# At the end of a sandwich layer: sums of squares by TensorE, products with high parts first, low parts after a half's updates

## The chip, the core and the metric

The kernel runs on one core of a Trainium2 chip. The metric is the device time of one execution in microseconds (us). An execution has one instruction queue for each engine: TensorE (PE) multiplies, VectorE (DVE) and ScalarE (ACT) work element by element, GpSimd (POOL) does a few additions and small powers, and SyncE (SP) issues most of the transfers. The engines wait for each other through semaphores. An engine takes its queue in order, so an instruction that waits holds up all those behind it.

## The reference, cut to what matters

The program is a chain of eight layers on x, 512 tokens of 1024 features in float32. The last four layers are "sandwiches", and the change is in how they end:

```python
def rmsnorm(x, g):
    y = x32 * lax.rsqrt(jnp.mean(x32 * x32, axis=-1, keepdims=True) + RMS_EPS)
    return (y * g.astype(jnp.float32)).astype(x.dtype)

def sandwich(x, g_pre, g_post, fn):
    return x + rmsnorm(fn(rmsnorm(x, g_pre)), g_post)
```

They are m0 (attention and convolution), f0 (feed-forward), m1 (attention and state space) and f1 (feed-forward). So the end of a layer needs a sum of squares of its own output over all 1024 features, then the update of x, and then, for the next layer, a sum of squares of the new x.

## The kernel before, in words

All of x lies in SBUF as eight tiles of 128 features by 512 tokens (`xs[0]` to `xs[7]`). A float32 product is made of three faster ones: a weight panel W is held as a high part `wh` and a low part `wl`, an activation as `xh` and `xl` (or `yh` and `yl`), and `mm3` adds wh·xh, wh·xl and wl·xh into the same PSUM tile (in the trace these are the products named g<-xh,wh, g<-xl,wh and g<-xh,wl). `panel` does that for the eight feature tiles k: 24 products for one weight panel of 128 output features.

Weight panels lie in the pool `pw`: three buffers each for `wh` and `wl`. `wchunk` takes a buffer and loads a panel; a panel that was split in an earlier layer comes by two transfers of SP, `wh<-preh` and `wl<-prel`. A transfer starts when the last reader of the old panel in its buffer is done.

`sandwich_end` (line 965) is the end of a layer. Its last three output panels are made in two halves of 256 tokens (`one`, `two`), so that the norm of half one can be worked out while half two is multiplied. In the order of the code, which PE and DVE keep here (`pinned[0] = (PE, V)`):

- `SumSq` collects the squares: ACT squares a tile (line 466), POOL adds it to `acc` (line 470), the last tile stays apart, and `sums` lets PE add over the 128 features with products of one column, a<-ones,acc and a<-ones,t.
- `factor` makes 1/sqrt from it, `diagonal` and `spread` bring it onto all partitions by two products a<-t,ones.
- `update(m, t, b)` scales the output tile, adds it to x on DVE, has ACT make `xh` (line 549), notes the square for later, and has DVE make the `xl` of the update before (`low`).
- The first three panels of the next layer, W0, W1 and W2, are multiplied with X in halves: W0 and W1 in turn for each k (`two_panels`), then W2. W0 to W2 are fetched as the buffers of this layer's last three panels come free.
- `panel_and_scales` (line 383) fetches W3 with the next free buffer, multiplies it for all 512 tokens, and makes the scale of the next norm after its first four k.

The last sandwich, f1, has no next layer (`srcs is None`): its updates go straight to the output.

Of the kernel before, what the change touches and what calls it, by code (L numbers as in the profile page):

```python
# [4 lines left out]
P = 128  # L5
NT = 512
D = 1024
KD = D // P
# [171 lines left out]
def build(nc, tc, A, out, stages=("a0", "b", "c", "a1", "m0", "f0", "m1", "f1")):  # L180
# [6 lines left out]
    AF = mybir.ActivationFunctionType  # L187
# [3 lines left out]
    V, S, G, PE = nc.vector, nc.scalar, nc.gpsimd, nc.tensor  # L191
# [3 lines left out]
    class Ordered:  # L195


        def __init__(self, eng):
            self.eng = eng
# [8 lines left out]
    PE, V = Ordered(PE), Ordered(V)  # L208
# [8 lines left out]
    def tl(pool, shape, tag, dt=F32, **kw):  # L217
        uid[0] += 1
        return pool.tile(list(shape), dt, tag=tag, name=f"{tag}_{uid[0]}", **kw)

    with ctx:
        pc = newpool(ctx, "pc")
# [22 lines left out]
        def psum_a():  # L245
            return tl(psa, (P, NT), "a")
# [206 lines left out]
        class SumSq:  # L453


            def __init__(self, n, apart=True):
                self.n, self.acc, self.rest, self.apart = n, None, {}, apart and n > 1

            def add(self, src, i, t=ALL, cls=False):
                if i == 0 and self.acc is None:  # L460
                    self.acc = tl(psm, (P, NT), "acc", bufs=1)
                sq = tmp() if i else self.acc
                if cls:
                    S.activation(classes(sq), tokens(src), AF.Square)
                else:
                    S.activation(sq[:, t], src, AF.Square)  # L466
                if i == self.n - 1 and self.apart:
                    self.rest[t.start] = sq
                elif i:
                    G.tensor_tensor(self.acc[:, t], self.acc[:, t], sq[:, t], op=ADD)  # L470

            def sums(self, t=ALL):

                ps = psum_a()
                n = (t.stop - t.start) // P
                for c in range(n):
                    o = t.start + c * P
                    both = [self.acc]
                    if self.apart:
                        both.append(self.rest[max(k for k in self.rest if k <= o)])  # L480
                    for i, a in enumerate(both):
                        PE.matmul(ps[:, c:c + 1], lhsT=a[:, o:o + P], rhs=ones[:, 0:1],
                                  start=i == 0, stop=i == len(both) - 1)
                return ps[:, 0:n]

        def small(n, tag):
            return tl(psm, (P, n), tag)

        neghalf = tl(pc, (P, 4), "neghalf")
        V.memset(neghalf, 0.5)  # L490
        S.activation(neghalf, neghalf, AF.Copy, scale=-1.0)
# [38 lines left out]
        state = {"first": None}  # L530

        def new_norm(row):
            state.update(row=row, X=[], ss=SumSq(KD, False))

        def finish_x(k, t=ALL, sq=True):

# [426 lines left out]


        def sandwich_end(W, Y, O, fresh, grow, srcs, pre=None, first=()):
            ss = SumSq(KD)
            kt = len(Y)
            nf = KD - 3

            def put(m, ps, t):  # L970
                if fresh:
                    ss.add(ps, m, t)
                    S.activation(O[m][:, t], ps, AF.Copy, scale=gcol(grow, m))
                else:
                    V.tensor_tensor(O[m][:, t], O[m][:, t], ps, op=ADD)
                    ss.add(O[m][:, t], m, t)
            first = list(first)
            for m in range(nf):
                put(m, first.pop(0) if first else gemm_T(W[m], Y), ALL)
            ch = [wchunk(W[m], kt * P) for m in range(nf, KD)]  # L980
            if pre is not None:
                s2 = small(4, "pc2")
                V.tensor_tensor(s2, pre, pre, op=MUL)

            def factor(t):
                c = small(2, "pc")
                if pre is None:
                    rstd(c, ss.sums(t), 1.0 / D, EPS)
                else:
                    a = slice(t.start // P, t.stop // P)  # L990
                    V.tensor_tensor(c, ss.sums(t), s2[:, a], op=MUL)
                    rstd(c, c, 1.0 / D, EPS)
                    V.tensor_tensor(c, c, pre[:, a], op=MUL)
                return c

            pss = {}

            def begin(m, t, k=None):
                pss[m] = psum_g()
                panel(pss[m], ch[m - nf], Y, t, range(kt if k is None else k))  # L1000

            def end(m, t, k):
                panel(pss[m], ch[m - nf], Y, t, range(k, kt))

            def done(m, t):
                put(m, pss[m][:, t], t)
            one, two = HALVES
            low, squares = [], []

            def add_squares():  # L1010
                while squares:
                    m, t = squares.pop(0)
                    state["ss"].add(xs[m][:, t], m, t)

            def update(m, t, b):
                o, x = O[m][:, t], xs[m][:, t]
                if fresh:
                    V.tensor_tensor(o, o, b, op=MUL)
                else:
                    V.scalar_tensor_tensor(o, o, gcol(grow, m), b, op0=MUL, op1=MUL)  # L1020
                (G if srcs is None and m % 3 == 2 else V).tensor_tensor(x, x, o, op=ADD)
                low.append(finish_x(m, t, False))
                if srcs:
                    squares.append((m, t))
                if len(low) > 1:
                    low.pop(0)()

            def last_low():
                low.pop(0)()
            a, b, c = range(nf, KD)  # L1030
            pinned[0] = (PE, V)
            for m in (a, b, c):
                begin(m, one)
                done(m, one)
            begin(a, two, kt - 4)
            f = factor(one)
            end(a, two, kt - 4)
            done(a, two)
            d1 = diagonal(f)
            if srcs:  # L1040
# [24 lines left out]
            ps = [psum_g() for _ in range(3)]  # L1065
            def two_panels(ks, t=one):
                for k in ks:
                    panel(ps[0], W0, X, t, [k])
                    panel(ps[1], W1, X, t, [k])
            two_panels(range(2))  # L1070
            update(4, one, b1)
            f = factor(two)
            update(5, one, b1)
            d2 = diagonal(f)
            add_squares()
            two_panels(range(2, 5))
            b2 = spread(d2)
            update(6, one, b1)
            update(7, one, b1)
            last_low()  # L1080
            add_squares()
            two_panels(range(5, KD))
            panel(ps[2], W2, X, one)
            for m in range(KD):
                update(m, two, b2)
                add_squares()
            last_low()
            two_panels(range(KD), two)
            panel(ps[2], W2, X, two)
            pinned[0] = (PE,)  # L1090
            p, sc, sb = panel_and_scales(srcs[3], X)
            state["first"] = ps + [p], sc, sb
            pinned[0] = ()
# [363 lines left out]
        def layer_m1(nxt):  # L1457
            with ExitStack() as c:
# [122 lines left out]
                V.tensor_tensor(t2[0:64], ps[64:128], t2[64:128], op=MUL)  # L1581
                V.tensor_tensor(kr[0:64], t1[0:64], t2[0:64], op=ADD)
                S.activation(kr[64:128], kr[0:64], AF.Copy)
                ss = SumSq(2)
                CQ = []
                for i in range(2):
                    ps = gemm_T(pre("m1_win", 4 + i), X)
# [165 lines left out]
```

## Time and profile before

| what | value |
|---|---|
| median of three runs | 2880.51 us (2877.24 to 2885.08) |
| the profiled execution | 2881.13 us, of which the span from the first to the last instruction is 2879.3 us |
| PE busy | 2812.2 us, 98% of the span |
| DVE, ACT, POOL busy | 1617.3, 1033.6, 215.4 us |
| mean granted TensorE clock | 0.991 |
| ends of m0, f0, m1, f1 in the trace | from about 1852, 2239, 2468 and 2848 us |

Starts are in us from the first instruction. A row of the timeline gives start, duration, engine, line, operation and tiles; in brackets stands how long the engine sat idle before it and what ended that. Durations of PE's rows overlap, since products are pipelined, so the distance between two starts tells what a product costs. A float32 product that isn't split stands as two rows (x2), and helpers record line 205 for most operations of PE and DVE, so the tile names tell which step it is. The granted clock is given as a share of full speed: TensorE has two levels, 1.2 and 2.4 GHz, and 0.51 to 0.57 in a short stretch means that the lower one held in nearly all of it.

### The profile page before, as it was taken

The page shows a single profiled execution, that of the slowest core. Times are in us where ns is not written, and L with a number is a line of the kernel's source. Part 1 is how long each engine was busy: PE and PEld are TensorE (multiplying, and loading weights), DVE is VectorE, ACT ScalarE, POOL GpSimd, SP SyncE. Part 2 cuts the span into 40 slices and gives each one's busy share as a digit, 9 for nine tenths or more (in the row PEclk, how much of TensorE's full clock was granted, in tenths as well). Part 3 has the DMA queues.
Part 4 walks back from the last instruction along what each step waited for, and adds up shares of the span by engine and source line. Part 5 has one row for each costly group of instructions (what it writes and reads, how often), then busy time and mean ns, then how long its engine had stood idle before and what let it go on. Part 6 is the DMA issues. An engine that isn't in the chain of part 4 may idle for free. (4 is left out here: it accounts for less than half of the span.)

```text
span 2879.3 us, 35015 instructions
## 1 busy us (share of the span) xinstructions
PE 2812.2 (98%) x13542; PEld 2320.6 (81%) x13542; DVE 1617.3 (56%) x3092; ACT 1033.6 (36%) x1661; POOL 215.4 (7%) x187
## 2 busy tenths in 40 slices
PE   8999999999999999999999998989999899999998
PEld 7888888888888888788888886778888756888886
DVE  4454654645455665654565488479754685343334
ACT  4322344444444432343323314443333325332222
POOL 2000010000000101220010100110000200200001
PEclk9999999999999999999999999999999999999999
DMA  4222332222222366555544352347773430423222
GB/s 157 95 88 95 121 109 96 81 88 95 74 96 89 128 205 207 183 191 161 160 163 161 123 193 94 114 171 257 278 254 106 170 137 19 143 92 101 97 94 68
DMA packets 127416, 385.48 MB, mean 134 GB/s; under 512 B 16144, under 2 KB 23057, under 8 KB 127249
## 3 DMA queue, kind: packets, MB, share of 16 engines
q1 hardware_dynamic: 107088, 325.57, 34.2%
q10 hardware_dynamic: 20160, 57.68, 5.4%
q8 instruction: 106, 1.74, 0.2%
q14 instruction: 62, 0.50, 0.1%
HBM read 312.94 MB, written 70.25 MB: 133 GB/s over the span
## 5 line engine op out<-in xcount | busy, mean ns | idle before, releaser
L320 ACT ACTIVATE wh<-wr 128x1024 fp32r<-128x1024 f32 (+2 forms) x408 | 421.6, 1034 | 1148.8 <-PE g L205 917.5
L205 DVE TENSOR_TENSOR wl<-wr,wh 128x1024 fp32r<-128x1024 f32 (+2 forms) x408 | 506.1, 1241 | 307.9 <-ACT wh L320 303.5
L205 PE MATMUL g<-xl,wh 128*128 128x512 f32 (+1 forms) x1720 | 659.1, 383 | 11.3 <-DVE xl L205 11.0
L205 PE MATMUL g<-xh,wh 128*128 128x512 f32 (+1 forms) x1720 | 662.9, 385 | 4.3 <-DMA wh<-preh 3.6
L205 PE MATMUL g<-xh,wl 128*128 128x512 f32 (+1 forms) x1720 | 657.4, 382 | 5.0 <-DMA wl<-prel 3.9
L205 PE MATMUL g<-yh,wh 128*128 128x512 f32 (+1 forms) x1046 | 393.4, 377 | 0.1
L205 PE MATMUL g<-wh,xh 128*128 128x512 f32 (+1 forms) x992 | 381.4, 385 | 9.8 <-ACT wh L320 9.8
L205 PE MATMUL g<-yl,wh 128*128 128x512 f32 (+1 forms) x1046 | 390.2, 373 | 0.0
L205 PE MATMUL g<-yh,wl 128*128 128x512 f32 (+1 forms) x1046 | 390.1, 373 | 0.0
L205 PEld LDWEIGHTS g<-xl,wh 128*128 128x128 f32 x1720 | 325.5, 189 | 75.5 <-DVE xl L205 15.3
L205 PEld LDWEIGHTS g<-xh,wl 128*128 128x128 f32 x1720 | 325.4, 189 | 69.6 <-DMA wl<-prel 4.9
L205 PEld LDWEIGHTS g<-xh,wh 128*128 128x128 f32 x1720 | 325.4, 189 | 65.8 <-DMA wh<-preh 4.6
L205 PE MATMUL g<-wl,xh 128*128 128x512 f32 (+1 forms) x992 | 376.7, 380 | 0.0
L205 PE MATMUL g<-wh,xl 128*128 128x512 f32 (+1 forms) x992 | 375.3, 378 | 0.0
L470 POOL TENSOR_TENSOR acc<-acc,t 128x256 f32<-128x256 f32 (+1 forms) x109 | 120.9, 1109 | 1721.4 <-issue 1406.9
L205 PEld LDWEIGHTS g<-yl,wh 128*128 128x128 f32 x1046 | 197.2, 189 | 36.1 <-issue 1.4
L205 PEld LDWEIGHTS g<-yh,wh 128*128 128x128 f32 x1046 | 197.0, 188 | 36.2 <-issue 1.4
L205 PEld LDWEIGHTS g<-yh,wl 128*128 128x128 f32 x1046 | 197.5, 189 | 34.3 <-DVE wl L205 0.4
L205 PEld LDWEIGHTS g<-wh,xh 128*128 128x128 f32 x992 | 187.7, 189 | 43.1 <-ACT wh L320 9.8
L205 PEld LDWEIGHTS g<-wh,xl 128*128 128x128 f32 x992 | 187.8, 189 | 34.3
L205 PEld LDWEIGHTS g<-wl,xh 128*128 128x128 f32 x992 | 187.9, 189 | 33.1 <-DVE wl L205 0.8
L205 DVE TENSOR_TENSOR t<-g,sb 128x512 f32<-128x512 f32 x112 | 77.1, 690 | 227.3 <-PE g L205 226.0
(309 smaller groups left out, 2679.1 us busy)
## 6 DMA issues: line engine op xcount, KB each, us to landing
wh<-preh SPq DMA_DIRECT2D x48, 512.0 KB, 3.8
wl<-prel SPq DMA_DIRECT2D x48, 512.0 KB, 4.3
wr<-in_f_wg_dram SPq DMA_DIRECT2D x40, 512.0 KB, 3.5
wr<-in_f_wu_dram SPq DMA_DIRECT2D x40, 512.0 KB, 3.5
preh<-ph ACTq DMA_DIRECT2D x39, 512.0 KB, 3.5
prel<-pl ACTq DMA_DIRECT2D x39, 512.0 KB, 6.5
wr<-in_a_wv_dram SPq DMA_DIRECT2D x32, 512.0 KB, 3.5
wr<-in_a_wu_dram SPq DMA_DIRECT2D x32, 512.0 KB, 3.7
```

The costliest lines, as they stand in the source:

```text
L205: r = f(*a, **k)
L320: S.activation(wh[:, :n], wr[:, :n], AF.Copy)
L470: G.tensor_tensor(self.acc[:, t], self.acc[:, t], sq[:, t], op=ADD)
```

## The change

Three things change at the sandwich ends.

- `SumSq(KD, 3)`: in the sum of squares of the layer's output, the last three tiles stay apart, not only the last one. PE's sum for 128 tokens then has four products of one column (acc and three tiles) where it had two.
- `PESums`: the squares of the new x are no longer added up by POOL. ACT squares each tile right after `xh`, and PE adds it at once: per tile and half two products of one column into one PSUM tile, which a product with `zeros` opens.
- `high` and `lows` take the place of `two_panels` and `panel`: for a half, all products with `xh` come first (for half one those of W0 and W1, then of W2; for half two all three panels in turn for each k), with the squares' products in between. `xl` is made only after all eight updates of the half, and all products with `xl` come last. All four remaining updates of half one stand ahead of the first product.

```diff
@@ class SumSq
-                if i == self.n - 1 and self.apart:
-                    self.rest[t.start] = sq
+                if i >= self.n - self.apart:
+                    self.rest.setdefault(t.start, []).append(sq)
@@
+        class PESums:
+            def __init__(self):
+                self.ps, self.n = psum_a(), 0
+                PE.matmul(self.ps[:, 0:4], lhsT=ones, rhs=zeros, start=True, stop=False)
+            def add(self, sq, t):
+                for o in range(t.start, t.stop, P):
+                    self.n += 1
+                    PE.matmul(self.ps[:, o // P:o // P + 1], lhsT=sq[:, o:o + P], rhs=ones[:, 0:1],
+                              start=False, stop=self.n == 4 * KD)
@@ def sandwich_end
-            ss = SumSq(KD)
+            ss = SumSq(KD, 3)
@@ def update
                 low.append(finish_x(m, t, False))
                 if srcs:
-                    squares.append((m, t))
-                if len(low) > 1:
-                    low.pop(0)()
+                    sq = tmp()
+                    S.activation(sq[:, t], x, AF.Square)
+                    squares.append((sq, t))
@@ the next layer's first panels
-            two_panels(range(2))
-            update(4, one, b1)
+            def high(t, ks, ns=range(3), sums=True):
+                for k in ks:
+                    for n in ns:
+                        for i in range(2):
+                            PE.matmul(ps[n][:, t], lhsT=W[n][i][:, k * P:(k + 1) * P], rhs=X[k][0][:, t],
+                                      start=k == 0 and i == 0, stop=False)
+                    if sums:
+                        state["ss"].add(*squares.pop(0))
+            def lows(t, ks):
+                for k in ks:
+                    for n in range(3):
+                        PE.matmul(ps[n][:, t], lhsT=W[n][0][:, k * P:(k + 1) * P], rhs=X[k][1][:, t],
+                                  start=False, stop=k == KD - 1)
+            state["ss"] = PESums()
+            for m in range(4, KD):
+                update(m, one, b1)
+            high(one, range(3), range(2))
             f = factor(two)
-            update(5, one, b1)
+            high(one, range(3, KD), range(2))
+            last_low(2)
             d2 = diagonal(f)
-            add_squares()
-            two_panels(range(2, 5))
+            high(one, range(2), [2], False)
             b2 = spread(d2)
-            update(6, one, b1)
-            update(7, one, b1)
-            last_low()
-            add_squares()
-            two_panels(range(5, KD))
-            panel(ps[2], W2, X, one)
+            high(one, range(2, KD), [2], False)
+            last_low(KD - 2)
+            lows(one, range(KD))
             for m in range(KD):
                 update(m, two, b2)
-                add_squares()
-            last_low()
-            two_panels(range(KD), two)
-            panel(ps[2], W2, X, two)
+            high(two, range(KD))
+            last_low(KD)
+            lows(two, range(KD))
```

PE's queue where the next layer's panels begin at the end of m0 (wh_14691 and wl_14692 are W0, wh_14738 is W1, xh_14725 and xl_14726 the first tile of the new x), before:

```order
L205 MATMUL g_14786<-xh_14725,wh_14691 128x256
L205 MATMUL g_14786<-xl_14726,wh_14691 128x256
L205 MATMUL g_14786<-xh_14725,wl_14692 128x256
L205 MATMUL g_14787<-xh_14725,wh_14738 128x256
L205 MATMUL g_14787<-xl_14726,wh_14738 128x256
L205 MATMUL g_14787<-xh_14725,wl_14739 128x256
```

and in the changed kernel (a_14796 is the PSUM tile of the sums, t_14731 the squares of the first tile, wh_14694 W0 and wh_14743 W1):

```order
L205 MATMUL a_14796<-zeros_112,ones_108 128x4
L205 MATMUL g_14793<-xh_14728,wh_14694 128x256
L205 MATMUL g_14793<-xh_14728,wl_14695 128x256
L205 MATMUL g_14794<-xh_14728,wh_14743 128x256
L205 MATMUL g_14794<-xh_14728,wl_14744 128x256
L205 MATMUL a_14796<-ones_108,t_14731 128x1 x2
```

The two products with xl have left this place, and two products of one column have come.

The last products of the stage and the first with W3 (wh_15049, 512 tokens), before. The row with wh_14691 or wl_14692 is the last use of W0's buffers, and W2 is wh_14782; between the dots stand 20 more products of W2:

```order
L205 MATMUL g_14786<-xl_14871,wh_14691 128x256
L205 MATMUL g_14786<-xh_14870,wl_14692 128x256
L205 MATMUL g_14787<-xh_14870,wh_14738 128x256
L205 MATMUL g_14787<-xl_14871,wh_14738 128x256
L205 MATMUL g_14787<-xh_14870,wl_14739 128x256
L205 MATMUL g_14788<-xh_14725,wh_14782 128x256
...
L205 MATMUL g_14788<-xh_14870,wh_14782 128x256
L205 MATMUL g_14788<-xl_14871,wh_14782 128x256
L205 MATMUL g_14788<-xh_14870,wl_14783 128x256
L205 MATMUL g_15053<-xh_14725,wh_15049 128x512
```

and in the changed kernel (W0, W1 and W2 are wh_14694, wh_14743 and wh_14789, W3 is wh_15076):

```order
L205 MATMUL g_14795<-xl_14815,wh_14789 128x256
L205 MATMUL g_14793<-xl_14822,wh_14694 128x256
L205 MATMUL g_14794<-xl_14822,wh_14743 128x256
L205 MATMUL g_14795<-xl_14822,wh_14789 128x256
L205 MATMUL g_15080<-xh_14728,wh_15076 128x512
```

Before, 28 products stand between the last read of W0's `wh` and the first one with W3; now there are two.

SP's queue at the same place, before (wh_15049 and wl_15050 are W3):

```order
L300 DMA pr_15212<-in_m_win_dram 128x1024
L316 DMA wh_15049<-preh_1533_7938 128x1024
L317 DMA wl_15050<-prel_1534_7939 128x1024
L254 DMA wr_15480<-in_f_wu_dram 128x1024
L254 DMA wr_15536<-in_f_wg_dram 128x1024
```

and in the changed kernel (wh_15076 and wl_15077):

```order
L300 DMA pr_15234<-in_m_win_dram 128x1024
L317 DMA wl_15077<-prel_1535_7941 128x1024
L316 DMA wh_15076<-preh_1534_7940 128x1024
L254 DMA wr_15502<-in_f_wu_dram 128x1024
L254 DMA wr_15558<-in_f_wg_dram 128x1024
```

The two transfers of W3 have changed places: the low part of W0 is now free first.

## Rows read from the trace of the kernel before

**Rows 1.** The page, part 1: busy time, share of the span, instructions.

```profile
PE 2812.2 (98%) x13542; PEld 2320.6 (81%) x13542; DVE 1617.3 (56%) x3092; ACT 1033.6 (36%) x1661; POOL 215.4 (7%) x187
```

**Rows 2.** PE's stage table, m0 then f0, m1: stretch, length, busy, clock.

```profile
1870.50:1897.10 26.60, 21.06 (x158) 1.00 0.27 95
1899.00:1903.00 4.00, 4.00 (x11) 0.57 0.95 297
2257.80:2261.20 3.40, 3.40 (x17) 0.51 0.16 64
2490.00:2497.00 7.00, 7.00 (x35) 0.52 0.17 65
2515.20:2519.00 3.80, 3.76 (x16) 1.00 0.68 245
```

**Rows 3.** Waits of PE in that stage: in total, times, longest.

```profile
PE g L205 <- DVE xl L205: 4.3, 6, 1.0
...
PE g L205 <- DVE xl L205: 4.1, 6, 0.8
...
PE g L205 <- DVE xl L205: 2.5, 4, 0.7
```

**Rows 4.** Timeline of PE: fetched panels, and the stage's borders.

```profile
1870.50 0.28 PE L205 MATMUL g<-xh,wh 128*128 128x256 f32 x1
1872.55 0.39 PE L205 MATMUL g<-xh,wl 128*128 128x256 f32 x1 [1.16 <-DMA wl<-prel]
1893.53 0.28 PE L205 MATMUL g<-xl,wh 128*128 128x256 f32 x1
1896.89 0.28 PE L205 MATMUL g<-xh,wl 128*128 128x256 f32 x1
1898.92 0.50 PE L205 MATMUL g<-xh,wh 128*128 128x512 f32 x1 [1.75 <-DMA wh<-preh]
2282.28 0.50 PE L205 MATMUL g<-xh,wh 128*128 128x512 f32 x1 [0.22 <-DMA wh<-preh]
2283.96 0.50 PE L205 MATMUL g<-xh,wl 128*128 128x512 f32 x1 [0.94 <-DMA wl<-prel]
2515.24 0.50 PE L205 MATMUL g<-xh,wh 128*128 128x512 f32 x1 [0.22 <-DMA wh<-preh]
```

**Rows 5.** Timeline of PE: one-column products at full and low clock; a spread.

```profile
1861.97 0.28 PE L205 MATMUL a<-ones,acc 128*128 128x1 f32 x2
1862.99 0.28 PE L205 MATMUL g<-yl,wh 128*128 128x256 f32 x1
1865.74 0.60 PE L205 MATMUL a<-t,ones 128*128 128x128 f32 x4
1866.10 0.36 PE L205 MATMUL g<-yh,wh 128*128 128x256 f32 x1
2490.58 0.42 PE L205 MATMUL a<-ones,acc 128*128 128x1 f32 x2
2492.14 0.56 PE L205 MATMUL g<-xh,wh 128*128 128x256 f32 x1
```

**Rows 6.** Timeline of SP: the transfer of W3's high part, in m0.

```profile
1893.85 0.32 SPq L316 DMA_DIRECT2D wh<-preh  x1
```

**Rows 7.** Timeline of DVE: an update; xl without and with POOL adding.

```profile
1866.38 0.42 DVE L205 TENSOR_TENSOR qkT<-qkT,a 128x256 f32<-128x256 f32 x1 [1.96 <-PE a L205]
1867.18 0.41 DVE L205 TENSOR_TENSOR qkT<-qkT,a 128x256 f32<-128x256 f32 x1
1875.35 0.48 DVE L205 SCALAR_TENSOR_TENSOR xl<-x,gains,xh 128x256 fp32r<-128x256 f32 x1
1877.35 0.94 DVE L205 SCALAR_TENSOR_TENSOR xl<-x,gains,xh 128x256 fp32r<-128x256 f32 x1
```

**Rows 8.** Timeline of POOL: additions into acc; of PE: f1's second sum.

```profile
1876.41 5.97 POOL L470 TENSOR_TENSOR acc<-acc,t 128x256 f32<-128x256 f32 x7 [0.98 <-POOL pc L498]
2863.95 0.38 PE L205 MATMUL a<-ones,t 128*128 128x1 f32 x2 [0.74 <-ACT t L466]
```

More of the change, by code (lines that the diff above doesn't have):

```diff
@@ L453, in build, with __init__ @@
         class SumSq:
-            def __init__(self, n, apart=True):
-                self.n, self.acc, self.rest, self.apart = n, None, {}, apart and n > 1
+            def __init__(self, n, apart=0):
+                self.n, self.acc, self.rest, self.apart = n, None, {}, apart
             def add(self, src, i, t=ALL, cls=False):
@@ L478, in sums @@
                     both = [self.acc]
-                    if self.apart:
-                        both.append(self.rest[max(k for k in self.rest if k <= o)])
+                    if self.rest:
+                        both += self.rest[max(k for k in self.rest if k <= o)]
                     for i, a in enumerate(both):
@@ L484, in sums @@
                 return ps[:, 0:n]
+        class PESums:
[7 more added lines that the diff above has]
+                              start=False, stop=self.n == 4 * KD)
+            def sums(self, t=ALL):
+                return self.ps[:, t.start // P:t.stop // P]
         def small(n, tag):
             return tl(psm, (P, n), tag)
+        zeros = tl(pc, (P, 4), "zeros")
+        V.memset(zeros, 0.0)
         neghalf = tl(pc, (P, 4), "neghalf")
@@ L532, in new_norm @@
         def new_norm(row):
-            state.update(row=row, X=[], ss=SumSq(KD, False))
+            state.update(row=row, X=[], ss=SumSq(KD))
         def finish_x(k, t=ALL, sq=True):
@@ L1007, in sandwich_end @@
             one, two = HALVES
[L1008 to L1013, printed above, removed]
+            low = []
             def update(m, t, b):
@@ L1023, in update, with last_low @@
                 if srcs:
-                    squares.append((m, t))
-                if len(low) > 1:
+                    sq = tmp()
+                    S.activation(sq[:, t], x, AF.Square)
+                    squares.append((sq, t))
+            squares = []
+            def last_low(n):
+                for _ in range(n):
                     low.pop(0)()
-            def last_low():
-                low.pop(0)()
             a, b, c = range(nf, KD)
@@ L1065, in sandwich_end @@
             ps = [psum_g() for _ in range(3)]
-            def two_panels(ks, t=one):
+            W = [W0, W1, W2]
+            def high(t, ks, ns=range(3), sums=True):
                 for k in ks:
-                    panel(ps[0], W0, X, t, [k])
-                    panel(ps[1], W1, X, t, [k])
-            two_panels(range(2))
-            update(4, one, b1)
+                    for n in ns:
[13 more added lines that the diff above has]
+            high(one, range(3), range(2))
             f = factor(two)
-            update(5, one, b1)
+            high(one, range(3, KD), range(2))
+            last_low(2)
             d2 = diagonal(f)
-            add_squares()
-            two_panels(range(2, 5))
+            high(one, range(2), [2], False)
             b2 = spread(d2)
-            update(6, one, b1)
-            update(7, one, b1)
-            last_low()
-            add_squares()
-            two_panels(range(5, KD))
-            panel(ps[2], W2, X, one)
+            high(one, range(2, KD), [2], False)
+            last_low(KD - 2)
+            lows(one, range(KD))
             for m in range(KD):
                 update(m, two, b2)
-                add_squares()
-            last_low()
-            two_panels(range(KD), two)
-            panel(ps[2], W2, X, two)
+            high(two, range(KD))
+            last_low(KD)
+            lows(two, range(KD))
             pinned[0] = (PE,)
@@ L1583, in layer_m1 @@
                 S.activation(kr[64:128], kr[0:64], AF.Copy)
-                ss = SumSq(2)
+                ss = SumSq(2, 1)
                 CQ = []
```

## The prediction

> **What bounds the kernel now.** The first view to read is the busy time by engine: PE works in 98% of the span [rows 1], so a change pays only where it takes idle time or products from PE, and every product that it adds counts in full unless PE would have stood idle there. The second is the table of stages [rows 2]: the stretch at the end of m0 in which the next layer's W0, W1 and W2 are multiplied is one of the few where PE isn't full, 21.06 us busy in 26.60. The third is the list of PE's waits in that stretch and in its counterparts of f0 and m1 [rows 3]: PE waits for `xl` from VectorE 6, 6 and 4 times, 4.3, 4.1 and 2.5 us in all. The fourth is the timeline [rows 4], which shows the waits for fetched panels: 1.16 us for W1's low part inside the stage of m0, and after the stage those for W3, 1.75 in m0, 0.22 and 0.94 in f0, 0.22 in m1. So the stage has two limits, VectorE's `xl` and the fetches, and the change speaks to the first.
>
> **What the waits for xl cost.** Idle time understates it, since a product is counted as busy until its modelled end and the stream of products has to start again. In m0 the stage lasts from 1870.50 to 1896.89 plus one product, 0.12: 26.51 us. Its work is 144 products of 256 tokens at 0.12 (17.3), four one-column products (0.9) and a spread (0.4), 18.6 in all. 26.5 less 18.6 is 7.9, of which W1's wait takes 1.4 (the start at 1872.55 stands about 1.4 us later than in an unbroken stream). The rest, 6.5, is what `xl` costs: 0.36 us a wait more than the 4.3 of the list. With the same addition f0 has 4.1 + 6 x 0.36 = 6.3 and m1 2.5 + 4 x 0.36 = 3.9. I take all of it as saved, 16.7 us: with `xl` at the end of each half, VectorE makes an update every 0.80 us [rows 7], and PE now takes 4 x 0.12 plus two squares' products at 0.22, 0.92 us, for a tile of half one, and 1.16 in half two, where six products stand before the squares. PE is then the slower of the two, and the `xl` of a half are ready before `lows` begins. That POOL stops adding speeds VectorE further (`xl` took 0.94 beside POOL's additions and 0.48 without them [rows 7, 8]), but once PE is the slower one, that buys nothing more.
>
> **What the added products cost.** For 128 tokens a sum now takes four one-column products where it took two: 4 more for each half's `factor`, 8 for an end. The squares of x take 2 for each of 8 tiles and 2 halves, 32, one more opens the PSUM tile, and the 4 of the old sum go: 37 more for each of m0, f0 and m1, 8 more for f1, 119 in all. Their price is in the trace [rows 5]: four of them and the product behind them take from 1861.97 to 1862.99, 1.02 us; less 0.12 for that product, 0.90, so 0.22 each, though a one-column product moves a single column. Two products of 128 columns (a<-t,ones) hold the queue from 1865.74 to 1866.10, 0.18 each: what is paid is not the columns. At the lower clock four take from 2490.58 to 2492.14, 0.39 each. I take 0.22: 37 x 0.22 = 8.1 us for an end, 24.4 for three. The bounds are 0.18 (20.0) and, if the lower clock holds, 0.39. Nothing hides them: without the waits for `xl` PE runs through. They are not spared by ScalarE's squares either, which it made before as well.
>
> Here a page says otherwise. The Trainium skill, "TensorE: Matmul & The Clock Gate", section "Back-to-back issue gap", gives a product of 1 to 64 columns about 60 cycles, 25 ns; two passes each would make 119 products 6.0 us, an estimate from that page. The rows show 0.22 us for one, so the row decides.
>
> **What the wait for W3 becomes.** W3's high part goes into W0's buffer, and its transfer starts when W0's `wh` has been read for the last time: at 1893.53 in m0, with the transfer issued at 1893.85 and the first product at 1898.92, 5.1 us later [rows 4, 6]. Between that last read and W3's first product stood 28 products, some 3.4 us, under which most of the transfer lay. After the change two are left, because the products with `xl`, which read `wh`, close the stage and take the three panels in turn. So 26 x 0.12 = 3.1 us of cover go, and the wait grows by as much at each of the three ends: to 4.8 in m0, 3.3 in f0 and m1. Behind the waiting transfer on SP's queue stand the next feed-forward panels, which have W3's own 24 products as cover. In f0 the wait for W3's low part goes (0.94 + 0.27 for the new start = 1.2), since W0's low part is now free before the high one. Together 3 x 3.1 - 1.2 = 8.1 us. The bounds: the transfers issued in the trace landed for PE 3.4 to 5.1 us after issue (those of f0 and m1, and m0), so a wait of 3 to 5.
>
> **What the clock does.** After the 1.75 us in m0 the granted clock was 0.57 for 4.0 us, so TensorE was at the lower of its two levels [rows 2, 4]; ten of the 512-token products stand 0.40 apart there instead of 0.23, which costs 1.6. After 0.22 in m1 it stayed at 1.00. A wait of over 3 us in f0 and m1 should then bring the same 1.6 there, 3.2 together; the bounds are nothing, and 3.5 each as in m1's first stretch (7.0 us at 0.52). The two stretches that are slow already, 2257.80 to 2261.20 and 2490.00 to 2497.00, follow waits for W0 and W1, which remain; I leave them as they are.
>
> **The last end.** f1 has 8 more small products. The first sum is delayed by about 0.7 beyond a short wait there, and moves the half two behind it. In the second, PE waits 0.74 for ScalarE's last square [rows 8]; what can be done before it is hidden, two products (0.4) are not. About 1.0 us.
>
> **The sum.** +24.4 - 16.7 + 8.1 + 3.2 + 1.0 = +20.0 us. By end: m0 8.1 - 6.5 + 3.1 = 4.7; f0 8.1 - 6.3 + 1.9 + 1.6 = 5.3; m1 8.1 - 3.9 + 3.1 + 1.6 = 8.9; f1 1.0. The profiled execution took 2881.13 us, 0.6 above the median of the three runs. 2881.1 + 20.0 = 2901.1; I forecast 2901. Its own range is 2891 (small products at 0.18, no new low clock, the transfer quick) to 2911 (a low stretch of 7 us each time, the fetch as late as in m0 everywhere).
>
> **The rivals.** A difference of under 0.3%, 8.6 us, can't be told from none here.
> - The small products cost almost nothing, because their loads go under the products around them. At no cost the sum is 20.0 - 24.4 - 1.0 = -5.4, 2876, and at half price +7.3, 2888: no difference. Against it: 0.22 in every sum of the trace; for it, that no sum of the trace stands between products with other weights as these do. 0.08. By the figure of the Trainium skill's page "TensorE: Matmul & The Clock Gate" it would be 2881, an estimate.
> - Faster: the small products are as good as free and, since PE no longer stands still in the stage, the clock keeps its upper level in f0 and m1. The stretches of 3.4 and 7.0 us then give back half of their length, 5.2, and the 3.2 after W3 don't come: 2876 - 8 = 2868. It needs a small product below 0.04 us; from there on it is faster by more than 0.3%. The waits that precede these stretches are fetches, which the change doesn't touch: 0.05.
> - The wait for W3 doesn't grow: its transfer lands under `lows`. Then 9.3 and 3.2 go: +7.5, 2889, on the border. Against it: the changed queue of SP has the high part behind the low one, and its buffer is read to the third product from the end. 0.08.
> - The lower clock holds through the stage, because nearly half of PE's time there goes into one-column products. For one end 144 products at 0.21, 41 small ones at 0.39 and a spread make 47 us in place of 27; half of the stage so at three ends is +30, 2931. For it: in m1 the low stretch of 7.0 us took in the sum of one-column products at its start [rows 2, 5]. Against it: the trace has the clock fall only behind waits. 0.07.
>
> **How the numbers follow.** The forecast has 0.72. Range: 2884 to 2914, which takes in the bounds, half of the third rival and leaves out the cheap products below and the slow clock above. Faster 0.05; same 0.17 (the first rival, half of the third, and 0.05 of the forecast's low end); slower 0.78.
>
> **What would show it.** In the changed profile: 119 more one-column products (238 rows more), standing 0.2 us apart; no wait of PE for `xl`; PE's wait for `wh<-preh` before the first 512-token product of W3 at 3 us or more in m0, f0 and m1, with the clock near 0.5 behind it; POOL without additions of 128x256. The stage from the first W0 product to the last of half two about 28 us long in m0. The forecast is wrong if the small products stand 0.05 apart, if W3 waits no longer than before, or if PE still waits for `xl`.

## The result and the profile after

The changed kernel takes 2911.51 us (median of six runs, 2908.19 to 2924.53), the kernel before in the same runs 2881.48; the ratio is 1.0116, 95% interval 1.0099 to 1.0132. The forecast was slower by 20 us, it became 30. The profiled execution has a span of 2906.4 us, 27.0 more than before (2906.37 and 2879.34).

The page of the changed kernel, part 1 (busy time, share, instructions), against [rows 1], and the first line of the list of PE's waits from 1865 to 2570 us (us in total, times, longest):

```profile
PE 2847.0 (98%) x13780; PEld 2361.4 (81%) x13780; DVE 1602.0 (55%) x3093; ACT 1032.6 (36%) x1661; POOL 170.4 (6%) x129
```

```profile
PE g L205 <- DMA wh<-preh: 11.8, 5, 3.4
```

238 rows more on PE (119 products of two rows), 58 additions fewer on POOL. PE's waits for `xl`, 16 in the kernel before [rows 3], are gone from the list, and the panels' high parts have taken the first place. PE is still busy in 98% of the span, so by this part nothing looks wrong: the loss shows only by stretches.

The table of stages shows where it lies. I take each end from the last product with `y` to W3's sixteenth product by its rows: the stage, the wait for W3 and what the clock does behind it. The columns are the stretch, its length, PE busy (instructions), the mean granted clock, DMA share, GB/s. Before (m0, f0, m1):

```profile
1870.38:1904.27 33.89, 26.60 (x175) 0.95 0.42 141
2253.27:2287.96 34.69, 27.66 (x182) 0.95 0.38 131
2486.66:2519.04 32.38, 27.96 (x176) 0.89 0.30 106
sum 100.96, PE 82.23; mean PE 27.41
```

and after:

```profile
1867.23:1908.53 41.30, 37.33 (x248) 0.83 0.29 99
2255.73:2303.28 47.55, 41.78 (x249) 0.75 0.32 114
2502.45:2546.05 43.60, 39.03 (x249) 0.80 0.25 87
sum 132.45, PE 118.15; mean PE 39.38
```

The three ends are 7.4, 12.9 and 11.2 us longer, 31.5 together. All the rest gave 4.5 back, 3.2 of it ahead of m0's end, where the two kernels differ only in the first sum of that end. The clock's mean fell from 0.95, 0.95, 0.89 to 0.83, 0.75, 0.80. The same view of m0's end in four pieces tells when (answering to the first line of [rows 2]):

```profile
1867.40:1872.60 5.20, 4.26 (x36) 1.00 0.75 284
1872.60:1886.20 13.60, 13.60 (x65) 0.50 0.00 1
1886.20:1901.90 15.70, 15.70 (x134) 1.00 0.20 68
1901.90:1905.00 3.10, 0.07 (x2) 1.00 0.51 169
```

For 13.6 us, 0.50 stands beside a PE that is busy all the time: the lower of the two levels. In f0 it is 20.4 us, in m1 13.6. In the kernel before the stages had 0, 3.4 and 7 [rows 2]. PE's timeline (start, duration, tiles) shows what stood there: the start of the third tile and then the fall to the lower level, a tile of half two at the full one, and W3's first products with their waits:

```profile
1870.72 0.36 PE L205 MATMUL g<-xh,wh 128*128 128x256 f32 x1
...
1871.64 0.36 PE L205 MATMUL a<-ones,acc 128*128 128x1 f32 x2
1871.86 0.81 PE L205 MATMUL a<-ones,t 128*128 128x1 f32 x6
1872.53 0.49 PE L205 MATMUL a<-ones,acc 128*128 128x1 f32 x2
1872.89 1.42 PE L205 MATMUL a<-ones,t 128*128 128x1 f32 x6
1874.17 0.56 PE L205 MATMUL g<-xh,wh 128*128 128x256 f32 x1
1875.17 0.85 PE L205 MATMUL a<-ones,t 128*128 128x1 f32 x4
1875.88 0.56 PE L205 MATMUL g<-xh,wh 128*128 128x256 f32 x1
...
1896.52 0.36 PE L205 MATMUL g<-xh,wh 128*128 128x256 f32 x1
1897.31 0.50 PE L205 MATMUL a<-ones,t 128*128 128x1 f32 x4
1897.68 0.36 PE L205 MATMUL g<-xh,wh 128*128 128x256 f32 x1
...
1904.98 0.50 PE L205 MATMUL g<-xh,wh 128*128 128x512 f32 x1 [3.03 <-DMA wh<-preh]
2298.11 0.50 PE L205 MATMUL g<-xh,wh 128*128 128x512 f32 x1 [3.15 <-DMA wh<-preh]
2540.91 0.50 PE L205 MATMUL g<-xh,wh 128*128 128x512 f32 x1 [3.42 <-DMA wh<-preh]
```

The four rows from 1871.64 on are the second sum: eight one-column products in one run, four of them at the full clock (0.89 us) and four already slower (1.64). The two products of the third tile's squares stand right in front of them, so with these the run is ten long. A tile of half one (four products of 256 tokens, two of one column) then takes 1.71 us, from 1874.17 to 1875.88; ahead of the run it took 0.92, from 1870.72 to 1871.64. So a us at the lower level loses 0.79/1.71 = 0.46. A tile of half two, with six products and the same two, takes 1.16 from 1896.52 to 1897.68: 6 x 0.12 + 2 x 0.22. The price of the small products was as forecast; their effect on the clock wasn't. In m0 and m1 the clock fell while the run was being worked off (1872.6; 2507.5, the run from 2507.14); in f0 it fell ahead of it, at 2258.3, in a wait of 1.95 for W1, so there the run can't have started it.

### The profile page after: what moved, and what is told of

It reads as the page before. It is cut to its first block, busy times and chain, and to the rows that moved or that the text cites. A ratio compares the mean times of both kernels' runs of the same rounds, so it can differ in the third digit from the quotient of the medians.

```text
span 2906.4 us, 35393 instructions
## 1 busy us (share of the span) xinstructions
PE 2847.0 (98%) x13780; PEld 2361.4 (81%) x13780; DVE 1602.0 (55%) x3093; ACT 1032.6 (36%) x1661; POOL 170.4 (6%) x129
## 4 chain that ended last, share of the span: by engine, by line
PE 91%; DVE 5%; DMA 1%; ACT 1%; POOL 1%; issue 0%; SPq 0%; ACTq 0%; DVEq 0%; POOLq 0%
PE g L205 82%; PE a L205 9%; DVE cv L205 1%; DVE t L205 1%; DMA wl<-prel 0%; POOL pad L928 0%; DVE wl L205 0%; DVE s L205 0%; DMA wh<-preh 0%; DMA pr<-in_m_wab_dram 0%; DVE o L205 0%; ACT wh L320 0%; DVE qk L205 0%; DVE x L205 0%; POOL last L928 0%
## 5 line engine op out<-in xcount | busy, mean ns | idle before, releaser
L205 PE MATMUL g<-xh,wh 128*128 128x512 f32 (+1 forms) x1720 | 670.6, 391 | 12.6 <-DMA wh<-preh 11.8
L205 PE MATMUL g<-xl,wh 128*128 128x512 f32 (+1 forms) x1720 | 633.3, 381 | 0.0
L205 PEld LDWEIGHTS g<-xh,wh 128*128 128x128 f32 x1720 | 331.2, 193 | 74.0 <-DMA wh<-preh 12.9
L205 PEld LDWEIGHTS g<-xl,wh 128*128 128x128 f32 x1720 | 314.6, 189 | 60.3 <-issue 0.2
L470 POOL TENSOR_TENSOR acc<-acc,t 128x512 f32<-128x512 f32 x51 | 75.9, 1488 | 1689.3 <-issue 1425.8
```

The source lines that it names most:

```text
L205: r = f(*a, **k)
```

## The experiments

"Ends" is the sum of the three stretches above, read in the profiled execution of each kernel. The times need it beside them: in the middle of m0, from 1775 to 1845, where the code of all kernels is the same, the clock was low for 7 us (b2) to 34 us (e4, g2) in the profiled executions, and m0's last product with `y` came between 1865.60 (b2) and 1880.24 (e1). So up to 15 us between two times can come from there. One execution of each kernel was traced; how much of the spread of a single kernel's times, 16 us in the changed one, it makes isn't shown.

The ratios are to the kernel before in the same series, whose medians were 2880.7 to 2883.7; the other medians are of 4 to 12 executions. e2, e7 and g2 came out about 3 us above their forecasts; e4, e1 and e8 lie above both of theirs, by 5, 15 and 16. Of each edit the lines that matter are shown.

| run | median us | ratio to before (95%) | ends us |
|---|---|---|---|
| before | 2881.5 | | 101.0 |
| after | 2911.5 | 1.0116 (1.0099 to 1.0132) | 132.5 |
| e1_pool_squares | 2904.8 | 1.0074 (1.0056 to 1.0093) | 113.4 |
| e2_wide_sums | 2898.4 | 1.0057 (1.0039 to 1.0074) | 116.4 |
| e3_dense_half_two | 2923.8 | 1.0140 (1.0119 to 1.0160) | 136.3 |
| e4_w0_lows_first | 2916.3 | 1.0111 (1.0092 to 1.0130) | 130.1 |
| b1_before_pe_sums | 2892.7 | 1.0042 (1.0026 to 1.0058) | 113.9 |
| e7_pool_w0first | 2897.6 | 1.0062 (1.0043 to 1.0082) | 109.4 |
| e8_cover | 2903.5 | 1.0079 (1.0060 to 1.0098) | 115.1 |
| e9_cover_apart1 | 2898.9 | 1.0066 (1.0050 to 1.0081) | 111.6 |
| f1_filler | 2913.5 | 1.0118 (1.0100 to 1.0136) | 130.0 |
| b2_before_wide_sums | 2881.6 | 1.0003 (0.9991 to 1.0016) | 98.9 |
| f2_wide_cover | 2890.6 | 1.0029 (1.0015 to 1.0042) | 103.7 |
| g1_factor_wide | 2897.1 | 1.0064 (1.0040 to 1.0088) | 115.2 |
| g2_filler_factor_wide | 2897.4 | 1.0056 (1.0040 to 1.0072) | 115.0 |
| g3_dense_run_two | 2939.7 | 1.0205 (1.0184 to 1.0227) | 154.8 |

**The order without the sums (e1).** `state["ss"].add(xs[m][:, t], m, t)` on POOL again, no `PESums`:

```diff
-                    if sums:
-                        state["ss"].add(*squares.pop(0))
```

> The changed kernel, but the squares of the new x are added by POOL again as before, so 33 products of TensorE go at each of three ends; the order (high parts first, low parts after a half's updates) and the four-product sums stay. Theory A (the dense one-column products keep TensorE at its lower clock: 13.7, 20.5 and 13.7 us at the three ends, 10 in the kernel before): the products' 21.8 us go and the low stretches shrink to those of before, another 17; about 2873. Rival B (the waits for W0's and W1's panels lower the clock and it stays low for its time whatever follows): the low stretches stay at 13 to 20 us, only 21.8 go; about 2890. In either case PE's waits for xl stay away; if they come back the time is 5 to 10 higher.

Ends 113.4: 19 us of the 31.5 are gone, the waits for `xl` stay away; PE waits 1.6 us for ScalarE's `xh` instead. In the stage the clock was low for 0, 10.2 and 6.8 us. The time is far above both forecasts of it, partly by the middle of m0 (a mean clock of 0.78 between 1775 and 1845 against 0.90 before). The other part lies in the ends, which still lose 12: W3's waits were 3.93, 4.70 and 3.38 us, with a low clock at each, and the four-product sums stayed, 24 one-column products at 0.22 or 5.3 us in the three ends. So this run doesn't show what the order alone costs.

**The same sums, 128 columns wide (e2).** The opening product with `zeros` goes too.

```diff
-                    PE.matmul(self.ps[:, o // P:o // P + 1], lhsT=sq[:, o:o + P], rhs=ones[:, 0:1],
-                              start=False, stop=self.n == 4 * KD)
+                    PE.matmul(self.ps[:, o:o + P], lhsT=sq[:, o:o + P], rhs=ones,
+                              start=first, stop=self.n == 4 * KD)
```

> The changed kernel with each one-column product of the new sums made 128 columns wide: the same 96 products with the same weights, each giving the same sum in 128 columns; the opening product with zeros goes. By the spread's rows a product of 128 columns holds PE for 0.18 us, as long as one of one column (0.22), so PE's work is the same to 4 us. Theory A (few columns per time lower the clock): the low stretches shrink to those of before, 2890 to 2895. Rival B (waits lower it): they stay, 2907 to 2911. A third, that weights loaded so often lower it, also says 2907 to 2911.

Two rows of PE, one tile of half two apart, and the ends:

```profile
1890.58 0.61 PE L205 MATMUL a<-ones,t 128*128 128x128 f32 x4
1891.74 0.61 PE L205 MATMUL a<-ones,t 128*128 128x128 f32 x4
```

```profile
1870.26:1906.81 36.55, 32.57 (x246) 0.95 0.38 127
2257.40:2299.86 42.46, 34.93 (x247) 0.88 0.47 169
2498.97:2536.32 37.35, 32.54 (x247) 0.95 0.30 101
sum 116.36, PE 100.05; mean PE 33.35
```

A tile takes 1.16 us as with one column: the wide product costs nothing more. The products and their weight loads are the same but for the opening one, yet the ends get 16 us shorter and the clock is back at 0.95, 0.88, 0.95. What remains low in m0 and m1 stands behind the wait for W3. So the clock depends on how wide the squares' products are, at the same time for each, and not on how often weights are loaded.

**Half two as dense as half one (e3).**

```diff
-            high(two, range(KD))
+            high(two, range(KD), range(2))
+            high(two, range(KD), [2], False)
```

> The changed kernel with half two ordered like half one: W0's and W1's products with the high parts and the sums for all eight tiles first (4 products of 256 tokens and 2 of one column for a tile, where there were 6 and 2), then W2's. No fetch is waited for there. If the density of one-column products alone pulls the clock down, half two has about 10 us at the lower level at each end, 4.6 each: about 2925. If they only keep down a clock that a wait has lowered, nothing changes: 2908 to 2914.

The stretch of half one and that of half two in m0:

```profile
1880.00:1897.00 17.00, 17.00 (x82) 0.51 0.05 19
1897.00:1911.00 14.00, 14.00 (x122) 1.00 0.25 76
```

Half two runs at 1.00 although its tiles are the same as those that ran at 0.50. The density alone doesn't lower the clock: something in half one does first. The time, 12 us above the changed kernel's, says the opposite of the trace: in the profiled executions 3.9 of it lie in the ends (the low stretch of half one is 3.4 longer in m0 and in m1), and 9.3 ahead of them, where the clock was low for 31 us of the middle of m0 against 14. Read by its time alone, this run would have confirmed the wrong theory.

**W3's cover (e4, e7).** e4 has the last low products panel by panel, W0's first; e7 is that with e1:

```diff
-            lows(two, range(KD))
+            for n in range(3):
+                lows(two, range(KD), [n])
```

> The changed kernel with the last products (low parts of half two) panel by panel, W0's eight first, so that W0's high buffer is free 16 products before the end instead of 2. My theory of the wait for W3 (3.0, 3.2 and 3.4 us in the changed kernel): it shrinks by 14 products at 0.12, 1.7 us, at each end, and the low clock behind it in f0 and m1 may go, 1.5 each: 2903 to 2906. Rival: the transfer is late for another reason (its queue): 2911.

> Squares added by POOL and the last products panel by panel, W0 first, in the changed kernel's order. The squares on POOL left 113 us in the three ends (101 before), of which the waits for W3 were 12.0 and the low clock behind them some 5; W0 first shortened such waits by 0.3 to 0.9 and kept the clock up behind them. So 104 to 108 in the ends, 2886 to 2895. If the wait for W3 isn't what is left of the loss, it stays at 2900 to 2905.

SP's queue in e4, m0:

```profile
1907.95 0.32 SPq L317 DMA_DIRECT2D wl<-prel  x1
1909.83 0.32 SPq L316 DMA_DIRECT2D wh<-preh  x1
```

and W3's first product:

```profile
1914.14 0.50 PE L205 MATMUL g<-xh,wh 128*128 128x512 f32 x1 [2.43 <-DMA wh<-preh]
```

The wait fell by 0.6 (0.3 in f0, 0.9 in m1), not by 1.7. In the changed kernel `wh` was issued 3.6 us behind `wl` (1898.19, 1901.75) and used 3.2 us later; here it goes out 1.9 behind `wl`, while that is still on its way (3.4 us from issue to landing), and is used after 4.3. I read that as the two transfers slowing each other, which no run tests; most of the gain is spent on the later landing. The clock stayed up behind the shorter waits in f0 and m1. e7 came to 109.4 in the ends and 2898, 4 us less than e1 by the ends.

**The sums without the order (b1, b2).** The old order, with the squares on PE behind each tile's six products of W0 and W1; b2 has them 128 columns wide:

```diff
                     panel(ps[0], W0, X, t, [k])
                     panel(ps[1], W1, X, t, [k])
+                    if done_sq:
+                        state["ss"].add(*done_sq.pop(0))
```

> The kernel before with one part of the change alone: the squares of the new x go to TensorE as one-column products, two behind the six products of W0 and W1 for each tile and half (96 products in three ends); order and low parts as before, no opening product. In the ends (stage and the first 15 products of W3) the kernel before takes 101 us by the trace and the changed one 132. Theory: 21 us of products less what the waits for xl cost (16.7), which they fill: 2885 to 2890 if the clock stays, up to 2900 if products of one column this dense (two behind six) hold the clock down after the waits for W0 and W1 as two behind four do. Rival (POOL's additions were what held VectorE and with it PE): faster than before, 2875 or less.

> The kernel before with the squares of the new x summed by TensorE in its old order, as in b1, but each product 128 columns wide as in e2. b1 took 114 us in the three ends with 41 us at the lower clock, and 10 are left there if wide products don't hold it down, which is worth some 13: 99 to 102 in the ends, 2878 to 2883, no difference from before. If the low stretches stay: 112 to 114, 2890 to 2893.

b1, the same three stretches, and the sum of b2's:

```profile
1866.70:1902.59 35.89, 34.63 (x239) 0.86 0.30 104
2251.25:2290.09 38.84, 36.34 (x239) 0.82 0.30 103
2488.31:2527.52 39.21, 37.78 (x239) 0.78 0.25 84
sum 113.94, PE 108.75; mean PE 36.25
```

```profile
sum 98.88, PE 93.10; mean PE 31.03
```

In b1 no wait for `xl` is left, and for W3 only 0.63 us for its low part in f0, but the clock is low for 10.2, 13.7 and 17.1 us. In b2, the same kernel with wide products, it is low for 6.8 us in f0 alone, and the 96 products (21 us by their price) cost nothing: they fill the time in which PE waited for VectorE (no wait for `xl` is left in it either). The ends are 2 us shorter than before, and the times can't be told apart.

**More cover for W3 (e8, e9, f2).** e8 has POOL's squares and, in half two, the low parts of half one beside W0's and W1's products, W2's products last; e9 has the old sum with two products. f2 has e2's wide sums and this half two:

```diff
-            high(two, range(KD))
+            high(two, range(KD), range(2))
             last_low(KD)
-            lows(two, range(KD))
+            high(two, range(4), [2], False)
+            lows(two, range(KD), [0])
+            lows(two, range(KD), [1])
+            high(two, range(4, KD), [2], False)
+            lows(two, range(KD), [2])
```

> Squares added by POOL; half one in the changed order, but its low parts wait for half two, where each tile has 3 of them, then W0's and W1's high products of the tile and the low products of the tile before; W2's 24 products for half two come last, so W0's buffer is free 24 products before W3's first. Theory (the order wins what the waits for xl cost, and loses it by W3's cover and the one-column products): ends of 93 to 97 us against 101 before, 2875 to 2879. Rival: VectorE paces half two, and the waits for xl come back, 4 an end: 2883 to 2888.

> The kernel of e8_cover with the old sum of the layer's output (one tile apart, two products for 128 tokens): 8 one-column products fewer at each end, 1.8 us at the full clock, at f1 too, so 5 to 7 faster than e8_cover if nothing waits for POOL's last additions; up to 5 slower if PE waits for them at each end.

> The changed kernel with wide sums (e2, 116 us in the ends, of which the waits for W3 were 10.9) and another order in half two: W0's and W1's high products with the sums, four tiles of W2's, the low products of W0, then of W1, then the rest of W2, so that W0's buffer is free 24 products before W3's first, nearly as in the kernel before. If the lost cover of W3 is what is left of the loss, the waits for W3 fall below 3 us together and the clock stays up behind them: 104 to 107 in the ends, 2884 to 2888. If the low products come to wait for VectorE's xl instead: 109 to 112, 2889 to 2893.

e8's waits of PE over the three ends, and the sum of f2:

```profile
PE g L205 <- ACT xh L567: 10.1, 10, 3.2
PE g L205 <- DMA wh<-preh: 8.3, 6, 3.8
```

```profile
sum 103.65, PE 94.51; mean PE 31.50
```

My theory for e8 fell: with the low parts moved out of half one, PE reaches half two before its first updates, and waits 10.1 us for ScalarE's `xh`. e9 was 3.5 us shorter in the ends and 5 in time; eight products fewer at each end would give 5.3. f2 did what was asked of it: waits for W3 of 0.37, 2.17 and 0.82, 13 us less than e2 in the ends, though 2891 is above its forecast and, by 0.3%, still slower than before.

**What lowers the clock (f1, g1, g2, g3).** f1 has 20 unread products in front of the first panel; g1 has the output's own sums wide (`rhs=ones` in `sums`, where it sums a half of 256 tokens), so the run of eight above is no longer narrow; g2 is both; g3 is e3 with a run of eight put into half two:

```diff
+            for _ in range(20):
+                PE.matmul(ps[2][:, one], lhsT=X[0][0][:, 0:P], rhs=X[0][0][:, one], start=True, stop=True)
             high(one, range(3), range(2))
```

```diff
             high(two, range(3), range(2))
+            for i in range(8):
+                PE.matmul(dull[:, 0:1], lhsT=ones, rhs=ones[:, 0:1], start=True, stop=True)
             high(two, range(3, KD), range(2))
```

> The changed kernel with 20 products of 256 tokens that nobody reads in front of the next layer's first panel at the three ends, 2.4 us each, so that TensorE works on while W0 and W1 are fetched (waits of 0.9, 2.6 and 1.2 us there). What is asked is why the dense one-column products run at the lower clock in half one (13.7, 20.5 and 13.7 us) and at the full one in half two, in the same density. If the waits for W0 and W1 lower the clock and the dense products only keep it down, the low stretches go nearly altogether: about 22 us won, 2 lost, 2890 to 2895, ends of 112 us against 132. If the long run of one-column products itself lowers it (the 8 of the second sum among them), they stay: 2912 to 2916.

> The changed kernel with the products of the output's own sums (eight for half two, which stand in one run behind the first three tiles of half one, and eight for half one) made 128 columns wide; the 32 of the squares of x keep one column. If the run of eight is what lowers the clock there (it fell within two us of that run with and without the waits for W0 and W1), m0's and m1's low stretches go (13.7 each) and f0's, which fell behind a wait of 1.95 before the run, stays or shrinks: 10 to 14 us won, 2898 to 2902, ends of 119 to 123 us against 132. If the squares' own products lower it, 13 to 20 us stay at each end and the time stays at 2909 to 2912.

> As g1, with the 20 unread products of f1 in front of the first panel too, so that neither a wait for W0 or W1 nor a run of one-column products stands ahead of the dense part. If each of the two lowers the clock and the dense products only hold it down, no low stretch is left in the stage of any of the three ends: ends of 112 to 114 us, 2890 to 2894. If the dense products lower it by themselves: low stretches of 10 or more, ends of 126 or more, 2905 to 2912.

> The kernel of e3 (half two as dense as half one, at the full clock there) with a run of eight one-column products that nobody reads behind the third tile of half two, as the second sum stands in half one. If the run is the trigger, the clock falls behind it and stays low through the other five tiles: 6 to 10 us at the lower level at each end in half two, 1.8 us for the run, 4 for the clock, about 17 more than e3 in the ends (136): 150 to 155. If half two keeps the full clock: 141 to 143.

f1 in m0, from the first unread product on:

```profile
1877.50:1884.20 6.70, 6.70 (x61) 1.00 0.63 224
1884.20:1898.00 13.80, 13.80 (x67) 0.51 0.00 0
```

PE works without a break, the run of eight lasts from 1882.88 to 1885.00, and the clock falls at 1884.2 all the same. So the waits aren't needed for the fall, as I had thought they were. In f0 filling them, all but 0.64 us, shortened the low stretch from 20.4 to 10.2, and it now begins behind the run. g1, the three ends:

```profile
1871.86:1906.66 34.80, 31.00 (x248) 1.00 0.33 118
2254.55:2297.55 43.00, 37.12 (x248) 0.84 0.38 137
2496.68:2534.09 37.41, 32.69 (x248) 0.95 0.30 101
sum 115.21, PE 100.82; mean PE 33.61
```

With the run wide and all 32 products of the squares still narrow and dense, no low stretch is left in the stages of m0 and m1 (m1's 0.95 is 3.4 us behind W3), and 6.8 us in f0, behind its waits of 1.85 and 0.87 for W1. g2, where 0.54 us is left of those waits, has none in any of the three stages; its unread products cost what it wins. And g3, m0's half two, with the run at 1895.0:

```profile
1892.00:1899.50 7.50, 7.50 (x67) 0.98 0.21 72
1899.50:1906.00 6.50, 6.50 (x31) 0.50 0.27 81
```

A run of the same length, put where e3 had the full clock, is followed by the lower level: 6.8, 10.2 and 13.7 us in half two of the three ends, which are 18.5 us longer than e3's. So the run between narrow squares makes the clock fall, shown by undoing it (g1, g2) and by making it (g3). e2 has the same run of eight between wide ones, and no low stretch in the stages of m0 and m1. Without any squares on PE it comes out both ways: e1 has none in m0, e7 has one of 3.4 us there, right behind its run (1875.04 to 1876.75) and 3.1 behind a wait of 1.31:

```profile
1877.00:1880.40 3.40, 3.40 (x18) 0.50 0.00 0
```

So whether the fall needs the narrow squares stays open. With them behind the run the stretch is longer, 13.6 us in m0 of the changed kernel for 3.4 here, but by themselves they don't keep a low clock down: in g1's f0, where it fell at the waits, it rose at 2266.5 while their tiles went on, 0.92 us apart (products at 2267.29, 2268.21, 2269.13 and 2270.05). In the changed kernel the clock came back when W2's products followed, with no sums between them. In b1 a tile's two and the old sum's four made a run of six, at the end of which the clock fell in m0 and m1, though there with a wait of 1.2 and 1.0 us shortly before; what it takes at least stays open.

## Why the prediction had the direction right and the clock wrong

By the steps of the forecast, in the profiled ends (m0, f0, m1):

- The new products less the waits for `xl`: forecast 1.6, 1.8 and 4.2, together 7.7. Measured, taking from the growth up to W3's first product (9.2, 13.4, 9.9) the change of the waits for W0, W1 and W3 and the added low clock at 0.46: 1.9, 1.6 and 4.0, together 7.5. With a small product at 0.22, as the rows above show it, the waits for `xl` were worth what the forecast said.
- The wait for W3: forecast +3.1 three times, 9.3. Measured +1.3, +2.9, +3.2, together 7.4. The mechanism was right; in m0 I had the transfer as late as before, 5.1 us from issue to product [rows 4, 6], and it took 3.2, issued when no other transfer moved anything (0 GB/s up to 1902.6).
- The waits for W0 and W1 were to stay: +0.4 in all.
- Behind W3: forecast +2.0 (low clock 3.2, less 1.2 for the low part). Measured -1.0: the low stretch came in f0 and m1, 3.4 us each, but m0's old one of 4.0 [rows 2] went, behind a longer wait than before.
- f1's end: forecast 1.0. Measured about 0.7, from its last product of 512 tokens (2847.54 before, 2873.83 after) to the end of the span.
- **The step that failed is "What the clock does".** It left the stages as they were. They got 13.6, 20.4 and 13.6 us at the lower level for 0, 3.4 and about 7, which cost 6.3, 7.8 and 3.1: 17.2 us that the sum didn't have. Making the output's sums wide and nothing else (g1) takes as much out of the ends, from 132.45 to 115.21. The smaller misses take 5.0 of it back, which leaves an excess of 12.2 in the four ends; the rest of the kernel, forecast unchanged, was 5.2 shorter in the profiled execution. The median lies 10 above the forecast.

That 2911.5 still lies inside 2884 to 2914 is luck: the range was said to leave out the slow clock, and the slow clock came; the misses the other way kept the time inside.

The rival "the lower clock holds through the stage" named this and had 0.07, because "the trace has the clock fall only behind waits". In the kernel before the stages had one run of four narrow products and no others; the change made it eight and put it between dense narrow ones, so that trace couldn't speak for it. Nor were the waits the only thing ahead of its falls: in f0 the run of four lasted from 2256.96 to 2257.77 and the clock fell at 2257.80 [rows 2], 1.8 us behind the last wait (2256.02):

```profile
2256.96 0.28 PE L205 MATMUL a<-ones,acc 128*128 128x1 f32 x2
```

The rival's reason, the share of time in one-column products, was near the truth but not it: e3 has that share at the full clock in half two, and the run (m0, m1) or a wait (f0) starts the fall. Its price, +30, took half of each stage at the lower level, by its own 47 us some 23.5; it was 13.6, 20.4 and 13.6, and 10.4 of these were there before.

The other rivals are out: the small products aren't cheap (0.22 each, as in the sums before), so the kernel isn't faster by them either, and the wait for W3 does grow. The page "TensorE: Matmul & The Clock Gate" of the Trainium skill, section "Back-to-back issue gap", gave 25 ns for a product of few columns, its weight load not counted; the runs again show 0.22 us for these float32 ones with theirs.

## What to carry to other kernels

Price short products twice: by their time and by the granted clock of everything that stands behind them, and read that clock by stretches, since PE's busy share was 98% in both kernels. Where a product may have any number of columns, try it 128 wide: here that cost no time and gave back 16 and 17 us in the ends (e2, g1). When an order is changed, count the products between the last read of a buffer and the first use of its next content; 26 of them at each of three ends were worth 7.4 us. Winning back both that cover and the waits for `xl` wasn't enough: f2 has no wait for `xl` and 3.4 us for W3 in all, b2 no wait for `xl` and 0.62 for W3, and neither is faster than the kernel before. The added products took what the waits had cost.

## What the runs showed of the hardware

- The granted clock went from 1.00 to 0.50 while TensorE was busy without a break (f1, 1884.2), in a run of eight one-column products among others of one column; with either the run (g2) or the others (e2, m0 and m1) 128 columns wide it didn't. What exactly the chip looks at stays open.
- A float32 product of 128 columns costs no more than one of a single column: tiles of 1.16 us in the changed kernel and in e2.
- A wait of 3.03 us for W3 (m0, changed kernel) left the clock at 1.00, one of 1.75 (m0, before) was followed by 3.4 us at the lower level: the length of a wait alone doesn't tell.
